# A convolution block on one core: all held tiles as native fp32 products, a grouped first norm, twelve convolution tiles on TensorE and the output gate's modulation on VectorE

## The chip, the cores and the metric

The kernel runs on one core of a Trainium2 chip. The metric is the device time of one execution in microseconds. TensorE (PE) multiplies, VectorE (DVE), ScalarE (ACT) and GpSimd (POOL) do elementwise work, SyncE (SP) issues nearly all DMA transfers. Each engine works through its own instructions in order.

## The reference

One decoder layer in fp32 for 256 positions of width 2048 (batch 1); the layer's mixer is the convolution, so the attention mixers of the reference do not run. Cut to what is computed:

```python
cond = silu(c)
mod = cond @ mod_w + mod_b                       # 6 x 2048 numbers
sh1, sc1, g1, sh2, sc2, g2 = split(mod, 6)
h = rms_norm(x, norm1_g) * (1 + sc1) + sh1
a, gt = split(h @ w_in + b_in, 2)                # 2048 -> 2 x 2048
u = a * sigmoid(gt)
u = depthwise_causal_conv(u, dw_w) + dw_b        # 31 taps along the sequence, each channel for itself
u = silu(layer_norm(u, ln_g, ln_b))
x = x + (1 + g1) * (u @ w_out + b_out)
h = rms_norm(x, norm2_g) * (1 + sc2) + sh2
x = x + (1 + g2) * (square(relu(h @ w1)) @ w2)   # 2048 -> 8192 -> 2048
```

## The kernel before

Channels lie on the 128 partitions (`P`), positions (`T` = 256) along the free axis; a vector of 2048 channels is 16 tiles of 128 (`KT`). Weights arrive in pieces of 1 MiB (128 x 2048 fp32), each loaded once, in the order of the list `order`, through a ring of five buffers named `raw` (`RAW`). `take(key)` (L182) hands out the next piece and issues the load that has room now; all loads stand in one queue on SP, so a load whose buffer is not free holds up those behind it. An order within an engine is set by a scheduler that works with a modelled time line; `urgent()` raises an instruction's priority and `issue_after` puts one behind another.

**Products.** Most of the matmul work is done as three products in the reduced type fp32r. `split_w` (L191) copies a weight half to `hi` on ACT (L200) and makes `lo = w - hi` on DVE or POOL (L201); the ring of `hi` and `lo` holds six halves, a job uses four. `mm` (L211) then multiplies `hi` with the activations' high and low part side by side (512 columns, L223) and `lo` with the high part (256 columns, L224). A *native* product instead multiplies fp32 by fp32 in one call (two records of the trace each).

**Stages.** `jobs` lists 16 in-projection jobs (`in`, a pair of a and gate tiles each), 8 out-projection jobs (`out`) and 4 x (8 `up` + 8 `down`) for the MLP.

1. *The first norm and the held tiles.* Squares of x on ACT (L433), 16 sums over channels by products with a matrix of ones (`column_sum`, L319), then an inverse root (`rms_factor`, L335). The first eight in-jobs are not done job by job: their 16 output tiles are *held* in all of PSUM, and the loop over the input tile k (L506) adds one input tile to all 16. Step k needs the modulation's scale and shift columns for k (`mod_col`, L294: one DVE instruction over 128 x 2048 that multiplies a piece of `mod_w` by `cond` and sums, L299) and one piece `first`. Steps in `NATIVE` (ten of 16) use native products (L486); in the six others `first_hi` and `first_lo` (L452, L466) split the piece on ACT and DVE, and three products follow (L490 to L492). `act_low` (L501) makes the low part of the activations for the later jobs.
2. *In-jobs 8 to 15.* Each is 32 pairs of `mm` calls. Beside them the depthwise convolution runs. A tile on DVE takes 31 multiply-adds (`tap`, L552), drawn from a stream by `advance(n)` with the counts of `ADVANCE`. A tile in `PE_TILES` goes to TensorE: `copy_wide` (L637) makes 16 shifted copies of 32 partitions each, on ACT or shared with DVE, `make_diag` (L650) builds small diagonal matrices on POOL, and `pe_conv` (L661) runs 32 products in 32-column groups, four side by side (L669). `CONV_AT` names the job behind which a tile is convolved, `COPY_AT` the job in which it is copied; the rings of copies and diagonals hold two tiles. Here also the modulation's `G1` and `SC2` parts are computed on TensorE as *row chunks* (`mod_chunk`, L232; 16 for each part, four for each of the first jobs by `LATE_IN`), and `mod_finish` (L281) turns the rows into columns by small products (L288).
3. *The tail of the convolution and the layer norm.* `stats` sums the convolved tiles and their squares on TensorE (L614); `find_shift` (L598) takes out a common mean estimated from two tiles; tile 15 is convolved last (L771), and mean and factor follow (L800 to L807).
4. *Out-jobs and the MLP*, ending with the store.

POOL makes the `lo` halves of the in-jobs (and of two out-jobs), DVE those of the rest.

```python
37  NATIVE = (1, 3, 5, 6, 8, 9, 11, 12, 14, 15)
44  PE_TILES = (0, 1, 2, 9, 10, 12, 14, 15)
45  CONV_AT = {9: (0,), 10: (1,), 11: (2,), 12: (9,), 13: (10,), 14: (12,), 15: (14,)}
46  ADVANCE = {7: 24, 8: 34, 9: 34, 10: 34, 11: 34, 12: 32, 13: 37, 14: 99}
51  LATE_IN = [0] * 8 + [4, 4, 4, 4, 4, 3, 3, 6]
299 nc.vector.scalar_tensor_tensor(w, w, 1.0, cb, op0=ALU.mult, op1=ALU.mult, accum_out=acc)
486 step = nc.tensor.matmul(p, parts_of[:, j, :], h, start=begin, stop=end, skip_group_check=True)
```

## Time and profile before

| what | value |
|---|---|
| median of 3 runs | 1124.56 us (1124.52 to 1125.03) |
| the profiled execution, its own time | 1122.33 us |
| its span | 1120.5 us, 17425 instructions |
| PE busy | 1098.4 us (98%) |
| DVE busy | 768.0 us (69%) |
| ACT busy | 582.0 us (52%) |
| POOL busy | 166.6 us (15%) |
| read from HBM | 290.14 MB |

The span is the stretch between the first and the last recorded event; the execution's own time holds 1.8 us more. A row of a time line or of a group gives start, duration, engine, source line, operation, the tile written and the tiles read with partitions x elements, and in brackets how long the engine had stood idle and what released it. Matmuls are pipelined: a record's duration holds its way through the array, so costs are taken from start to start.

### The profile page before, as it was taken

The page shows a single profiled execution, that of the slowest core. Times are in us where ns is not written, and L with a number is a line of the kernel's source. Part 1 is how long each engine was busy: PE and PEld are TensorE (multiplying, and loading weights), DVE is VectorE, ACT ScalarE, POOL GpSimd, SP SyncE. Part 2 cuts the span into 40 slices and gives each one's busy share as a digit, 9 for nine tenths or more (in the row PEclk, how much of TensorE's full clock was granted, in tenths as well). Part 3 has the DMA queues.
Part 4 walks back from the last instruction along what each step waited for, and adds up shares of the span by engine and source line. Part 5 has one row for each costly group of instructions (what it writes and reads, how often), then busy time and mean ns, then how long its engine had stood idle before and what let it go on. Part 6 is the DMA issues. An engine that isn't in the chain of part 4 may idle for free.

```text
span 1120.5 us, 17425 instructions
## 1 busy us (share of the span) xinstructions
PE 1098.4 (98%) x7088; PEld 946.6 (84%) x7088; DVE 768.0 (69%) x1025; ACT 582.0 (52%) x806; POOL 166.6 (15%) x103
## 2 busy tenths in 40 slices
PE   6999999999999999999999999999999999999998
PEld 4888776766699998888888888888888888888888
DVE  3988689987489989887765555555555665555653
ACT  5222395664675587554445554444655444555441
POOL 0000086467533262000000000000000000000000
PEclk8999999999999999999999999999999999999999
DMA  9999979888599977888775555555554655555640
GB/s 384 420 421 420 418 307 346 349 322 318 207 390 350 371 283 276 290 350 299 273 259 192 190 193 194 193 191 193 189 190 165 211 188 188 188 188 188 209 139 29
DMA packets 41553, 293.35 MB, mean 262 GB/s; under 512 B 4609, under 2 KB 5121, under 8 KB 6401
## 3 DMA queue, kind: packets, MB, share of 16 engines
q1 hardware_dynamic: 41328, 292.17, 70.4%
q8 instruction: 55, 0.90, 0.3%
q14 instruction: 24, 0.20, 0.0%
q10 hardware_dynamic: 146, 0.08, 0.0%
HBM read 290.14 MB, written 2.10 MB: 261 GB/s over the span
## 4 chain that ended last, share of the span: by engine, by line
PE 86%; DMA 6%; DVE 6%; ACT 1%; issue 0%; POOL 0%; DVEq 0%; ACTq 0%; POOLq 0%
PE mm L223 45%; PE mm L224 24%; DMA raw<-mod_c 4%; PE mm L220 3%; DVE raw L299 3%; PE mm L219 3%; PE mm L221 3%; PE row L241 2%; PE mm L669 2%; DMA raw<-w_in 1%; PE small L319 1%; DVE lo L470 1%; PE mm L111 1%; PE mm L486 1%; PE acc L669 0%
## 5 line engine op out<-in xcount | busy, mean ns | idle before, releaser
L200 ACT ACTIVATE hi<-raw 128x1024 fp32r<-128x1024 f32 x320 | 335.3, 1057 | 355.9 <-PE mm L223 327.1
L201 DVE TENSOR_TENSOR lo<-raw,hi 128x1024 fp32r<-128x1024 f32 x272 | 333.6, 1232 | 234.4 <-ACT hi L200 233.4
L223 PE MATMUL mm<-hl,hi 128*128 128x512 f32 x1184 | 414.3, 393 | 0.4 <-DVE u L686 0.4
L223 PE MATMUL mm<-u,hi 128*128 128x512 f32 x1056 | 366.8, 390 | 0.0
L224 PE MATMUL mm<-hl,lo 128*128 128x256 f32 x1184 | 332.2, 281 | 0.0
L224 PE MATMUL mm<-u,lo 128*128 128x256 f32 x1056 | 297.7, 282 | 0.0
L223 PEld LDWEIGHTS mm<-hl,hi 128*128 128x128 f32 x1184 | 221.6, 187 | 58.2 <-issue 8.4
L223 PEld LDWEIGHTS mm<-u,hi 128*128 128x128 f32 x1056 | 198.2, 188 | 41.7 <-DVE small L332 0.2
L224 PEld LDWEIGHTS mm<-hl,lo 128*128 128x128 f32 x1184 | 223.7, 189 | 5.1 <-issue 4.2
L224 PEld LDWEIGHTS mm<-u,lo 128*128 128x128 f32 x1056 | 199.6, 189 | 0.1
L299 DVE SCALAR_TENSOR_TENSOR raw<-raw,cond 128x2048 f32<-128x2048 f32 x64 | 148.3, 2320 | 20.3 <-DMA raw<-mod_c 14.7
L201 POOL TENSOR_TENSOR lo<-raw,hi 128x1024 fp32r<-128x1024 f32 x48 | 118.1, 2482 | 198.0 <-ACT hi L200 198.0
L561 DVE SCALAR_TENSOR_TENSOR acc<-u,v,acc 128x256 f32<-128x256 f32 x224 | 94.7, 490 | 1.9
L220 PE MATMUL mm<-hl,hi 128*128 128x256 f32 x288 | 81.5, 284 | 0.8 <-DVE hl L209 0.8
L219 PE MATMUL mm<-hl,hi 128*128 128x256 f32 x288 | 80.5, 284 | 1.2 <-ACT hl L208 0.8
L221 PE MATMUL mm<-hl,lo 128*128 128x256 f32 x288 | 81.1, 283 | 0.0
L219 PEld LDWEIGHTS mm<-hl,hi 128*128 128x128 f32 x288 | 54.6, 192 | 2.8 <-ACT hl L208 1.7
L220 PEld LDWEIGHTS mm<-hl,hi 128*128 128x128 f32 x288 | 55.2, 192 | 1.6 <-DVE hl L209 1.2
L221 PEld LDWEIGHTS mm<-hl,lo 128*128 128x128 f32 x288 | 55.2, 192 | 0.0
L646 ACT ACTIVATE wide<-u 32x284 f32<-32x284 f32 x110 | 48.2, 438 | 2.7 <-DVE u L686 1.4
L423 ACT ACTIVATE two<-mm 128x512 f32<-128x512 f32 x70 | 40.9, 584 | 13.5 <-PE mm L224 13.5
L523 ACT ACTIVATE two<-two,modc,amp 128x256 f32<-128x256 f32 x16 | 9.6, 599 | 71.2 <-DVE modc L279 71.2
(166 smaller groups left out, 916.7 us busy)
## 6 DMA issues: line engine op xcount, KB each, us to landing
raw<-w SPq DMA_DIRECT2D x128, 1024.0 KB, 4.9
raw<-mod_c SPq DMA_DIRECT2D x64, 1024.0 KB, 10.8
raw<-mod_r SPq DMA_DIRECT2D x32, 1024.0 KB, 7.9
raw<-w_in SPq DMA_DIRECT2D x16, 1024.0 KB, 7.2
raw<-w_out SPq DMA_DIRECT2D x16, 1024.0 KB, 7.4
first<-w_first SPq DMA_DIRECT2D x15, 1024.0 KB, 16.1
x<-x SPq DMA_DIRECT2D x2, 1024.0 KB, 6.9
x<-x SPq DMA_DIRECT2D x1, 2048.0 KB, 9.8
```

The source lines that it names most:

```text
L200: nc.scalar.activation(hi, w[:, ks, :], AF.Copy)
L201: end = engine.tensor_tensor(lo, w[:, ks, :], hi.bitcast(F32), op=ALU.subtract)
L219: nc.tensor.matmul(out_p, w, m[:, 0:T], start=begin, stop=False)
L220: nc.tensor.matmul(out_p, w, m[:, T : 2 * T], start=False, stop=False)
L221: state["mm_end"] = nc.tensor.matmul(out_p, lo[:, k % HALF, :], m[:, 0:T], start=False, stop=end)
L223: nc.tensor.matmul(p[:, c, :], hi[:, k % HALF, :], m, start=(k == 0), stop=(k == KT - 1))
L224: state["mm_end"] = nc.tensor.matmul(p[:, c, T : 2 * T], lo[:, k % HALF, :], m[:, 0:T], start=False, stop=(k == KT - 1), skip_group_check= ...
L241: state["row_end"] = nc.tensor.matmul(row_ps[0][32 * k : 32 * k + 32, :], cz[:, 4 * kg + k, 3 - b : 35 - b], w[:, 4 * k : 4 * k + 4, :], s ...
L299: nc.vector.scalar_tensor_tensor(w, w, 1.0, cb, op0=ALU.mult, op1=ALU.mult, accum_out=acc)
L423: nc.scalar.activation(t1, p[:, cs, T : 2 * T], AF.Copy)
L561: nc.vector.scalar_tensor_tensor(out, s, w, acc, op0=ALU.mult, op1=ALU.add)
L646: nc.scalar.activation(dst, src, AF.Copy)
```

## The change

- Every held tile uses native products; `first_hi`, `first_lo`, `NATIVE` and the split products go.
- The first norm's sum: half of the squares are made on DVE; the 16 sums go into four groups of 32 PSUM partitions, and one copy and one more product fold them. The first two columns are computed after the squares, and the inverse root's table is loaded earlier.
- `PE_TILES` grows from eight tiles to twelve: 0 to 2 and 7 to 15. DVE convolves tiles 3 to 6 only. `CONV_MID` sets three convolutions (1, 7, 13) into the middle of jobs 9, 10 and 15. The convolution's product is written into a free half of the PSUM tile `small` instead of an `mm` tile; the sums of `stats` move to an `acc` tile.
- `G1` is computed by 16 columns on DVE (`COLS_IN`, spread over jobs 8 to 14 between the taps); only `SC2` stays with row chunks (`ROWS_IN`: 1, 1, 1, 2, 2, 2, 1 and 6).
- `stats` for the first two groups of tiles come one job apart. The table of tap weights moves to a pool that is freed, and the pad grows by as much.

```diff
-NATIVE = (1, 3, 5, 6, 8, 9, 11, 12, 14, 15)
-GROUPS = [[4 * w + b for b in range(4)] for w in (G1, SC2)]
+GROUPS = [[4 * SC2 + b for b in range(4)]]
...
+COLS += [w * KT + k for w in (G1, SH2, G2) for k in range(KT)]
...
-PE_TILES = (0, 1, 2, 9, 10, 12, 14, 15)
-CONV_AT = {9: (0,), 10: (1,), 11: (2,), 12: (9,), 13: (10,), 14: (12,), 15: (14,)}
-ADVANCE = {7: 24, 8: 34, 9: 34, 10: 34, 11: 34, 12: 32, 13: 37, 14: 99}
+PE_TILES = (0, 1, 2, 7, 8, 9, 10, 11, 12, 13, 14, 15)
+CONV_AT = {8: (0,), 9: (2,), 10: (8,), 11: (9,), 12: (10,), 13: (11,), 14: (12,), 15: (14,)}
+CONV_MID = {9: 1, 10: 7, 15: 13}
+COPY_AT = {8: (0, 1), 9: (2, 7), 10: (8,), 11: (9,), 12: (10,), 13: (11,), 14: (12,)}
+ADVANCE = {7: 26, 8: 26, 9: 24, 10: 24, 11: 99}
 SHIFT = 2
-COPY_AT = {8: 0, 9: 1, 10: 2, 11: 9, 12: 10, 13: 12}
-PADDING = 8
-UNSHIFTED = 7
-LATE_IN = [0] * 8 + [4, 4, 4, 4, 4, 3, 3, 6]
+PADDING = 264
+ROWS_IN = {8: 1, 9: 1, 10: 1, 11: 2, 12: 2, 13: 2, 14: 1, 15: 6}
+COLS_IN = {8: 1, 9: 2, 10: 2, 11: 2, 12: 3, 13: 3, 14: 3}
...
-    dwq_sb = const.tile([P, 32 * len(PE_TILES)], F32, name="dwq_sb")
...
+    dwq_sb = early.tile([P, 32 * len(PE_TILES)], F32, name="dwq_sb")
...
+    table(AF.Abs_reciprocal_sqrt, cond[:, KT - 1, 0:1])
...
+    def rms_factor(total, ms, r, times=1):
+        by = 1.0 / (times * D)
+        nc.vector.tensor_scalar(ms, total, by, None, op0=ALU.mult)
+        return inverse_root(ms, total, by, r)
...
-    late = [("mod", nb, kg) for nb in ROWS for kg in range(4)] + [("col", SH2 * KT + k) for k in range(KT)]
+    rows_late = [("mod", nb, kg) for nb in ROWS for kg in range(4)]
+    late = [("col", w * KT + k) for w in (G1, SH2) for k in range(KT)]
...
-    quota = {("in", i): n for i, n in enumerate(LATE_IN)}
+    quota = {("in", i): n for i, n in COLS_IN.items()}
...
+    rows_of = {}
+    for n, job in enumerate(jobs):
+        n = ROWS_IN.get(n, 0)
+        rows_of[job], rows_late = rows_late[:n], rows_late[n:]
...
-        order += after[job]
+        order += rows_of[job] + after[job]
...
-    mods(by_col(0))
     p = ps.tile([P, 512], F32, name="small", bufs=1)
     for k2 in range(HALF):
         s = two()
-        nc.scalar.activation(s, pair_of(xs, k2), AF.Square)
-        column_sum(p[:, 0:T], [s[:, j, :] for j in range(2)], k2 == 0, k2 == HALF - 1)
-    r1 = tmp.tile([P, T], F32, name="r", bufs=1)
-    rms_factor(p[:, 0:T], p[:, T : 2 * T], r1)
-
-    root_end = state["root_end"]
+        if k2 < HALF // 2:
+            nc.scalar.activation(s, pair_of(xs, k2), AF.Square)
+        else:
+            nc.vector.tensor_tensor(s, pair_of(xs, k2), pair_of(xs, k2), op=ALU.mult)
+        for j in range(2):
+            g = (2 * k2 + j) % 4
+            nc.tensor.matmul(p[32 * g : 32 * g + 32, 0:T], ones[:, 0:32], s[:, j, :], start=k2 < 2, stop=k2 >= HALF - 2)
+    mods(by_col(0))
+    with urgent():
+        part = two()[:, 0, :]
+        nc.scalar.activation(part, p[:, 0:T], AF.Copy)
+        p = ps.tile([P, 512], F32, name="row", bufs=1)
+        nc.tensor.matmul(p[:, 0:T], ones, part, start=True, stop=True)
+        r1 = tmp.tile([P, T], F32, name="r", bufs=1)
+        rms_factor(p[:, 0:T], p[:, T : 2 * T], r1, 32)
...
-    first_parts = {}
-
-    def first_hi(k):
-        w = take(("first", k))
-        if k in NATIVE:
-            first_parts[k] = w
-            return
-        first_parts[k] = []
-        for h in range(2):
-            js = slice(h * HELD, (h + 1) * HELD)
-            hi = wts.tile([P, HALF, P], F32R, name="hi", bufs=6)
-            lo = wts.tile([P, HALF, P], F32R, name="lo", bufs=6)
-            with tc.issue_after(root_end):
-                nc.scalar.activation(hi, w[:, js, :], AF.Copy)
-            first_parts[k].append((hi, lo, w[:, js, :]))
-
-    def first_lo(k, h):
-        if k in NATIVE:
-            return
-        hi, lo, w = first_parts[k][h]
-        in_order(lambda: nc.vector.tensor_tensor(lo, w, hi.bitcast(F32), op=ALU.subtract))
...
     def first_mm(k, h):
+        w = take(("first", k))
         with tc.issue_after(state["step_end"].ins) if k else ExitStack():
-            parts_of = first_parts.pop(k)
-            m = hl[k // 2][:, k % 2, :]
             for n in range(HELD):
                 for c in range(2):
-                    p = held[n][:, c, :]
-                    j = 2 * n + c
-                    begin, end = k == 0 and c == 0, k == KT - 1
-                    if k in NATIVE:
-                        step = nc.tensor.matmul(p, parts_of[:, j, :], h, start=begin, stop=end, skip_group_check=True)
-                        continue
-                    hi, lo = parts_of[j // HELD][0:2]
-                    j %= HELD
-                    nc.tensor.matmul(p, hi[:, j, :], m[:, 0:T], start=begin, stop=False, skip_group_check=True)
-                    nc.tensor.matmul(p, hi[:, j, :], m[:, T : 2 * T], start=False, stop=False, skip_group_check=True)
-                    step = nc.tensor.matmul(p, lo[:, j, :], m[:, 0:T], start=False, stop=end, skip_group_check=True)
+                    step = nc.tensor.matmul(
+                        held[n][:, c, :], w[:, 2 * n + c, :], h, start=k == 0 and c == 0, stop=k == KT - 1, skip_group_check=True
+                    )
         state["step_end"] = step
...
-            first_lo(k - 1, 1)
-            if k - 1 not in NATIVE:
-                first_mm(k - 1, None)
...
-        first_hi(k)
-        if k in NATIVE:
-            first_mm(k, h)
+        first_mm(k, h)
...
-        for dst in (state["small"][:, T : 2 * T], state["shift"]):
-            nc.scalar.activation(dst, p, AF.Copy, scale=-1.0 / (SHIFT * P))
+        nc.scalar.activation(state["shift"], p, AF.Copy, scale=-1.0 / (SHIFT * P))
...
                 state["stats_end"] = nc.tensor.matmul(
-                    state["small"][32 * g : 32 * g + 32, 0:T], ones[:, 0:32], t, start=first, stop=m in last,
+                    state["sums"][32 * g : 32 * g + 32, :], ones[:, 0:32], t, start=first, stop=m in last,
...
     def stats(b):
+        if b == 0:
+            state["sums"] = ps_two()[:, 0, :]
...
-        p = ps.tile([P, 2, 2 * T], F32, name="mm", bufs=2)[:, 0, 0:T] if sq is None else ps_two()[:, 0, :]
+        p = state["small"][:, T : 2 * T] if sq is None else ps_two()[:, 0, :]
...
-            if ct == 14:
+            if HELD <= ct < KT - 1:
                 nc.vector.scalar_tensor_tensor(cv(ct), p, col("dwb", ct), state["shift"], op0=ALU.add, op1=ALU.add)
...
+    state["small"] = ps.tile([P, 512], F32, name="small", bufs=1)
     advance(ADVANCE[HELD - 1])
...
-        for ct in CONV_AT.get(n, ()) + ((15,) if n == KT - 1 else ()):
+        for ct in ((CONV_MID[n],) if n in CONV_MID else ()) + CONV_AT.get(n, ()) + ((15,) if n == KT - 1 else ()):
             make_diag(ct)
...
-        if n in COPY_AT:
-            copy_wide(COPY_AT[n], False)
+        for ct in COPY_AT.get(n, ()):
+            copy_wide(ct, False)
...
-            rows = list(after[job]) if i < KT - 1 else []
+            rows = list(rows_of[job]) if i < KT - 1 else []
             for c in range(2) if i < KT - 1 else (1, 0):
                 for ks in (range(HALF), range(HALF, KT)):
                     mm(p, c, job + (c,), hl, ks, i == KT - 1)
                     with tc.issue_after(state["mm_end"].ins):
                         mods(rows[:1])
                     del rows[:1]
+                    if n in CONV_MID and ks == range(HALF, KT) and c == (1 if i == KT - 1 else 0):
+                        with tc.issue_after(state["mm_end"].ins):
+                            pe_conv(CONV_MID[n])
...
-                if i >= KT - 2:
+                if i >= KT - 3:
                     copy_wide(i)
             if n == KT - 4:
                 add_shift(cvs[0], 4)
-                add_shift(cvs[1][:, 0:3, :], 3)
-            if n == KT - 2:
-                add_shift(cvs[2][:, 1:3, :], 2)
-            if n == KT - 1:
-                add_shift(cvs[3][:, 0:1, :], 1)
...
-                    mix(ct)
-            advance(ADVANCE.get(n, 0))
-            if n == KT - 2:
+                    pe_conv(ct)
+            if n == HELD + 1:
+                with tc.issue_after(state["conv_end"].ins):
+                    find_shift()
+            cols = list(after[job])
+            taps = ADVANCE.get(n, 0)
+            for left in range(len(cols), -1, -1):
+                m = taps // (left + 1)
+                advance(m)
+                taps -= m
+                mods(cols[:1])
+                del cols[:1]
+            if n == KT - 4:
+                add_shift(cvs[1], 4)
+            if n in (KT - 3, KT - 2):
                 with tc.issue_after(state["mm_end"].ins):
-                    for b in range(2):
-                        stats(b)
+                    stats(n - KT + 3)
...
-                nc.scalar.activation(sums, state["small"][:, 0:T], AF.Copy)
+                nc.scalar.activation(sums, state["sums"], AF.Copy)
```

25 lines of the change are left out of this document (5 added, 20 removed).

## The prediction

> **What bounds the kernel now.** I read the slices and queues of the page first, then busy time by stage, then the chain that ended last, and last the time lines of each engine around two borders: where the eight held tiles end (141 us) and where the convolution's tail begins (286 us). Columns of the first table: stretch, its length, busy time of PE, PEld, DVE, ACT and POOL with instruction counts, granted clock, DMA share, GB/s.
>
> ```profile
> span 1120.5 us, 17425 instructions
> core 0: us, PE busy (x) PEld busy (x) DVE busy (x) ACT busy (x) POOL busy (x), PEclk, DMA share, GB/s
> 4.00:128.00 124.00, 111.08 (x588) 95.66 (x587) 100.42 (x136) 38.18 (x60) 0.00 (x0) 0.97 1.01 420
> 128.00:141.00 13.00, 13.00 (x62) 11.44 (x61) 3.88 (x7) 6.19 (x10) 3.68 (x2) 1.00 1.02 417
> 141.00:286.00 145.00, 144.62 (x1179) 101.17 (x1178) 123.05 (x292) 93.30 (x167) 98.46 (x52) 1.00 0.82 316
> 286.00:308.00 22.00, 20.50 (x235) 12.02 (x234) 11.63 (x24) 15.58 (x31) 11.78 (x10) 1.00 0.67 254
> 420.00:1116.00 696.00, 696.00 (x4047) 616.58 (x4046) 427.79 (x458) 350.57 (x419) 7.40 (x3) 1.00 0.60 208
> ```
>
> There are three regimes. To 128 us the DMA engines are full (share 1.01, 420 GB/s) while PE has holes: this stage is paid in bytes. From 141 to 286 us PE is busy 144.62 of 145 us and DMA at 0.82: paid in TensorE work. The MLP from 420 us is PE alone, 696 of 696 us. The diff touches the first two; of the MLP it only moves addresses (the pad grows by the 256 elements that `dwq_sb` gave up), and I cost that at zero. The stretch 308 to 420 runs the same program from the same five `raw` buffers and I let it move as a block.
>
> **Front: all held tiles native.** Removed: six steps' ACT copies and DVE `lo` subtractions, and the waits for them. Bytes stay, so the question is how far PE ends behind the last byte.
>
> ```profile
> 124.97 0.38 PE acc L492
> 127.15 3.45 PE mm L486 x16
> 134.06 3.45 PE mm L486 x16
> 140.10 0.86 PE row L486 x4
> 286.29 3.59 PE mm L669 x64
> 109.18 2.29 DVE L299 SCALAR_TENSOR_TENSOR raw<-raw,cond 128x2048 f32<-128x2048 f32 x1 [1.57 <-DMA raw<-mod_c]
> 116.75 2.29 DVE L299 SCALAR_TENSOR_TENSOR raw<-raw,cond 128x2048 f32<-128x2048 f32 x1 [2.27 <-DMA raw<-mod_c]
> 123.70 1.22 DVE L470 TENSOR_TENSOR lo<-first,hi 128x1024 fp32r<-128x1024 f32 x1
> 127.64 2.29 DVE L299 SCALAR_TENSOR_TENSOR raw<-raw,cond 128x2048 f32<-128x2048 f32 x1
> 130.16 0.60 ACT L523 ACTIVATE two<-two,modc,amp 128x256 f32<-128x256 f32 x1 [5.23 <-DVE modc L279]
> ```
>
> The first five rows are the chain; the fifth, a whole convolution tile on PE (32 grouped products, two records each), is used further down. Step 13 is split and held by `lo` (123.70 on DVE), so its second half starts at 124.97; native step 14 starts at 127.15, step 15 at 134.06, and that ends at 140.10 + 0.86 = 141.0. A native step thus takes 134.06 - 127.15 = 6.9 us. The DVE rows that waited for DMA are the scale columns of steps 13 and 14: 7.57 us apart. That is the pace of delivery of 3 MiB, about 2.5 us each. 6.9 is below 7.5, so PE in native steps keeps pace, with 0.6 us a step to spare.
>
> Now the new end. Step 15's scale column lands at 116.75 + 7.5 = 124.3, its shift column 2.5 later, 126.8. Before, DVE began that column at 127.64, late, and `h` was ready at 130.16 + 0.60 = 130.8; the 0.8 us off makes it 129.9. Step 14's `h` comes 7.5 earlier, 122.4, its step runs to 129.3, so step 15 starts when `h` does: 129.9 + 6.9 = 136.8. **Gain 4.1 us.** What is late next are job 8's weights: behind the shift column stand 1 MiB of first weights, 0.7 of vectors and 1 MiB of w_in, 2.7 x 2.5 = 6.7 us, so 133.5. An estimate from the pace above; a copy and a subtraction must follow:
>
> ```profile
> 136.19 1.99 ACT L200 ACTIVATE hi<-raw 128x1024 fp32r<-128x1024 f32 x2
> 163.43 9.45 POOL L201 TENSOR_TENSOR lo<-raw,hi 128x1024 fp32r<-128x1024 f32 x4 [3.60 <-ACT hi L200]
> ```
>
> 1.0 for one `hi`, 9.45/4 = 2.4 for one `lo`: 136.9. I take **-4.0 us**. Bounds: zero if PE cannot hold 6.9 a step, -5 if step 15's bytes come 1 us early (the wait at 109.18 was 1.57).
>
> **Head: the first norm's sum.** Sixteen full sums become four groups side by side, half the squares go to DVE, a copy and one matmul fold them, and the table load moves ahead; DVE's first two columns stand behind its four squares, and SP's next loads behind those columns' buffers.
>
> ```profile
> 13.74 2.29 DVE L299 SCALAR_TENSOR_TENSOR raw<-raw,cond 128x2048 f32<-128x2048 f32 x1 [3.94 <-ACT cond L112]
> 9.63 9.88 PE L319 MATMUL small<-two,ones 128*128 128x256 f32 x32
> 20.06 1.28 ACT L326 ACT_TABLE_LOAD   x1 [5.31 <-DVE small L336]
> 25.61 0.80 PE L490 MATMUL mm<-hl,hi 128*128 128x256 f32 x2 [6.10 <-ACT hl L526]
> ```
>
> By the convolution tile, 32 grouped products of this width take 3.59 us, so sixteen take 1.8 of the 9.88, and the 1.28 goes; step 0 starts, as an estimate, 3 to 6 us before 25.61. The squares put ahead of DVE's columns cost nothing: the first column waited for `cond` until 13.74 anyway. The saving is **zero at the end**: it lies under the full DMA queue. It is cover, though: from 25.61, sixteen native steps end at 25.61 + 110.4 = 136.0, only 0.8 us before the bytes allow.
>
> **In stage: PE.** Sixteen row chunks (the G1 group) leave TensorE with their fold, four convolution tiles come. `mm` stays.
>
> ```profile
> 242.59 0.39 PE L223 MATMUL mm<-hl,hi 128*128 128x512 f32 x1
> 242.91 1.07 PE L241 MATMUL row<-raw,cz 128*32 128x512 f32 x8
> 243.91 0.39 PE L224 MATMUL mm<-hl,lo 128*128 128x256 f32 x1
> 234.85 0.50 PE L223 MATMUL mm<-hl,hi 128*128 128x512 f32 x1
> 242.24 0.40 PE L223 MATMUL mm<-hl,hi 128*128 128x512 f32 x1
> 242.47 0.28 PE L224 MATMUL mm<-hl,lo 128*128 128x256 f32 x1
> 224.02 0.79 PE row L288 x8
> ```
>
> A pair of `mm` matmuls takes (242.59 - 234.85)/22 = 0.352 us, a job of 32 pairs 11.3. From a 512-wide `mm` to its follower are 242.47 - 242.24 = 0.23 us in a plain run, so the chunk costs 243.91 - 242.59 - 0.23 = 1.09 us, not the 0.99 that a chain piece shows. Ahead of 286 us: 26 - 10 = 16 chunks x 1.09 = -17.4, the fold -0.8, and from six to ten convolution tiles, 4 x 3.6 = +14.4. **-3.8 us; I take -3.4**, since convolutions set into the middle of a job pay borders. The Trainium skill, "TensorEngine Tiling (Array Packing)", Key Properties, says that a change of tiling mode, not only of tile, drains TensorE. The trace agrees: 0.1 us a chunk above its bare time. By bare times the term would be 16 x 0.99 = 15.8, and the sum -2.2.
>
> **In stage: ACT, DVE, POOL.**
>
> ```profile
> 168.32 0.60 ACT L423 ACTIVATE two<-mm 128x512 f32<-128x512 f32 x1 [2.12 <-PE mm L224]
> 170.75 0.47 ACT L684 ACTIVATE two<-mm,v 128x256 f32<-128x256 f32 x1 [1.84 <-DVE mm L424]
> 173.66 0.47 ACT L677 ACTIVATE cv<-mm,v 128x256 f32<-128x256 f32 x1 [2.43 <-PE mm L669]
> 174.03 7.18 ACT L646 ACTIVATE wide<-u 32x284 f32<-32x284 f32 x16
> 144.84 5.58 DVE L561 SCALAR_TENSOR_TENSOR acc<-u,v,acc 128x256 f32<-128x256 f32 x14
> 24.00 2.22 DVE raw L299 x2
> 172.85 1.90 POOL L654 TENSOR_TENSOR diag<-v,dwq_sb 128x1024 f32<-128x1024 f32 x1
> ```
>
> DVE: four tiles less, 4 x 31 x 0.40 = -50; sixteen G1 columns, 16 x (2.22 + 0.2) = +39; tile 13's share of copies and the evacuations +7. Even. Its lateness holds `raw` buffers, hence SP's queue and the next weights, but five buffers reach a job ahead. ACT takes the load: 7.18 us for each copied tile, and five tiles (0, 1, 2, 7, 8) are due within jobs 8 to 10. PE needs there 3 x 11.3 + 3 x 1.09 + 5 x 3.6 = 55.2 us. ACT needs 5 x 7.18 = 35.9, three jobs' `hi` 12 x 1.0 = 12, the second pair of job 8 at 2.0, evacuations and gates 3 x 1.07 = 3.2, four convolution evacuations 1.9 and some held gates 2.5: 57.5 us. **+2 us**, bounds 0 and +19 (see the rivals). From job 11 one tile a job remains, and ACT has room. In the tail conv 14 and the sums still cover the copy of tile 15: zero.
>
> **Sum.** On the profiled execution, 1122.33 us with a span of 1120.5: -4.0 - 3.4 + 2.0 = -5.4, to 1116.9. The median of the runs, 1124.56, lies 2.2 above that execution, so 1119.2.
>
> **Rivals.**
> ACT hides its 2 us, because a late convolution is placed behind the next job's matmuls: for it speaks that `mm`'s two buffers are no longer shared with convolutions. 1124.56 - 7.4 = 1117.2.
>
> The front does not shorten: native steps lose 0.3 us each to jitter and PE ends at 141 as now. For it: only 0.8 us of cover without the head's gain. Against: the 6.9 is itself measured. 1123.2.
>
> The two-input lock. Here the trace shows:
>
> ```profile
> 313.50 2.29 DVE L299 SCALAR_TENSOR_TENSOR raw<-raw,cond 128x2048 f32<-128x2048 f32 x1 [0.74 <-PE mm L221]
> 314.49 6.91 POOL L201 TENSOR_TENSOR lo<-raw,hi 128x1024 fp32r<-128x1024 f32 x2 [4.33 <-ACT hi L200]
> ```
>
> Two `lo` in 6.91 us instead of 4.8, beginning while DVE ran a column: POOL stood until the column ended. If each G1 column holds POOL for 2.22 us, jobs 12 and 13 need 9.45 + 1.9 + 3 x 2.22 = 18.0 us of POOL against 11.3 + 2 x 1.09 + 3.6 = 17.1 of PE, job 14 18.0 against 16.0: +3.8 if no lead is left, 1123.0. The Trainium skill, "SBUF — State Buffer", section "SBUF: two separate sides", gives this as a rule: a DVE instruction with two SBUF inputs and a reading GpSimd one exclude each other for their whole length; the pair of rows above agrees. Against the price: POOL starts most jobs with `lo` already ahead.
>
> The slower side: ACT stays in order through its waits. In job 9 it stood 2.12 + 1.84 + 2.43 = 6.4 us for PE, for DVE's addition and for the convolution, when it had nothing else to do. Where all of it is demanded, the same stops in three jobs are 19.2 us. The point that decides: above 5.4 us of them (under a third) nothing is gained. At three fifths, +11.5: 1130.7.
>
> **How the numbers follow.** Forecast 0.45, ACT hidden 0.20, lock 0.10, front as before 0.08, ACT's stops 0.17. A difference under 0.2% (2.2 us) is about what runs of this kernel cannot tell from none. Forecast and hidden ACT are faster by more, 0.65; the lock and the unshortened front lie within it, 0.18; the stops are slower, 0.17. The range runs from 1115.0 (both bounds of the front and of ACT, with a little of the tail) to 1126.5, into the nearer part of the stops.
>
> **What would show it.** The step-15 group of native matmuls ends near 137 and the first `mm` of job 8 follows at once; DVE waits for `mod_c` in nearly every step from about 9 on; job 15's last `mm` lies near 281; the MLP keeps its length. Wrong: ACT's stops in jobs 8 to 10 with PE idle before L669; POOL `lo` means above 2.6; holes of PE ahead of L486 at the end of the front; an MLP longer by over 1 us, which I gave no cause for.

## The result, and the profile after

The kernel became slower: 1139.29 us (1135.98 to 1140.48) against 1124.80 us for the kernel before on the same chip, a ratio of 1.0109 with a 95% interval of [1.0064, 1.0154]. The forecast was 1119.2. The profiled execution of the changed kernel took 1140.48 us, its span is 1137.3 us.

The same table by stage, for the changed kernel. The stages end at other times now: the held tiles at 137.5, the in-stage at 298.

```profile
span 1137.3 us, 17448 instructions
core 0: us, PE busy (x) PEld busy (x) DVE busy (x) ACT busy (x) POOL busy (x), PEclk, DMA share, GB/s
4.00:128.00 124.00, 114.18 (x511) 93.49 (x510) 90.54 (x128) 25.19 (x46) 0.00 (x0) 0.97 1.01 420
128.00:137.50 9.50, 9.50 (x46) 8.28 (x44) 3.88 (x9) 5.30 (x11) 1.84 (x1) 1.00 1.03 421
137.50:298.00 160.50, 148.02 (x1305) 104.85 (x1307) 140.02 (x220) 116.24 (x219) 128.40 (x56) 0.98 0.77 294
298.00:320.00 22.00, 18.25 (x216) 9.99 (x216) 11.94 (x20) 13.38 (x28) 12.58 (x9) 1.00 0.61 215
434.00:1130.00 696.00, 694.68 (x4028) 614.57 (x4028) 427.92 (x459) 351.05 (x419) 7.85 (x4) 1.00 0.59 208
```

The front is shorter by 3.5 us (141.0 to 137.4). The in-stage, which was 145 us with PE idle for 0.4, is 160.5 us with PE idle for 12.5; POOL's busy time went from 98 to 128 us with 56 instructions against 52. From here on I measure to one mark, the first row product of the MLP's first job (L256 before, L258 after, 128 products in one row of the chain), and to the end. For the kernel before, the chain's row and the stretch from the held tiles to it:

```profile
406.97 3.63 PE row L256 x128
...
141.00:406.97 265.97, 263.10 (x2209) 209.73 (x2211) 225.91 (x408) 174.32 (x298) 144.67 (x79) 1.00 0.85 324
```

The same two for the changed kernel:

```profile
421.83 3.63 PE row L258 x128
...
137.50:421.83 284.33, 267.45 (x2330) 214.79 (x2332) 246.47 (x336) 197.15 (x349) 175.46 (x84) 0.98 0.82 308
```

The mark is 14.9 us later, the stretch behind it 2.0 us longer (715.5 against 713.5). Between the front and the mark PE is idle for 284.33 - 267.45 = 16.9 us, before for 2.9. Nearly all of the 14.9 us are lost ahead of the out-jobs: the first product of out-job 0 starts at 305.31 us before and at 319.49 us now, 14.2 us later, and from there to the mark it takes 101.7 and 102.3 us.

What grew is seen in the groups of the in-stage (137.5 to 300 us; mean ns behind the busy time), first of the kernel before:

```profile
L201 POOL TENSOR_TENSOR lo<-raw,hi 128x1024 fp32r<-128x1024 f32 x38 | 90.1, 2394 | 182.1 <-ACT hi L200 182.1
L644 DVE COPY wide<-u 32x284 f32<-32x284 f32 x18 | 8.4, 466 | 0.4
L561 DVE SCALAR_TENSOR_TENSOR acc<-u,v,acc 128x256 f32<-128x256 f32 x224 | 94.7, 490 | 1.9
```

Of the changed kernel, and as last row its one-element addition in the front (4 to 137 us), where POOL does nothing:

```profile
L203 POOL TENSOR_TENSOR lo<-raw,hi 128x1024 fp32r<-128x1024 f32 x37 | 107.2, 2923 | 165.8 <-ACT hi L202 165.7
L301 DVE SCALAR_TENSOR_TENSOR raw<-raw,cond 128x2048 f32<-128x2048 f32 x16 | 44.5, 2783 | 8.4 <-DMA raw<-mod_c 8.4
L281 DVE TENSOR_TENSOR modc<-modc,v 128x1 f32<-128x1 f32 x16 | 23.0, 1438 | 0.2
L618 DVE COPY wide<-u 32x284 f32<-32x284 f32 x19 | 11.5, 604 | 0.3
L536 DVE SCALAR_TENSOR_TENSOR acc<-u,v,acc 128x256 f32<-128x256 f32 x112 | 45.4, 479 | 0.0
...
L281 DVE TENSOR_TENSOR modc<-modc,v 128x1 f32<-128x1 f32 x16 | 2.5, 158 | 0.5
```

Adding one number to each partition takes 158 ns in the front and 1438 ns here. Columns take 2783 instead of 2290 ns, `lo` 2923 instead of 2394. The convolution's taps, whose accumulator lies in PSUM, are as before (479 and 490 ns). DVE's time line, and POOL's below it, show the pattern:

```profile
233.11 2.29 DVE L301 SCALAR_TENSOR_TENSOR raw<-raw,cond 128x2048 f32<-128x2048 f32 x1
235.44 2.22 DVE L281 TENSOR_TENSOR modc<-modc,v 128x1 f32<-128x1 f32 x1
237.59 2.28 DVE L301 SCALAR_TENSOR_TENSOR raw<-raw,cond 128x2048 f32<-128x2048 f32 x1
239.91 2.24 DVE L281 TENSOR_TENSOR modc<-modc,v 128x1 f32<-128x1 f32 x1
```

```profile
233.86 8.28 POOL L203 TENSOR_TENSOR lo<-raw,hi 128x1024 fp32r<-128x1024 f32 x2 [3.06 <-ACT hi L202]
```

POOL's first `lo` stands until the column ends at 235.4, and runs to 237.6; the addition, issued at 235.44, ends with it; then the next column runs, POOL's second `lo` stands, and the next addition ends with that. In this stretch the two engines take strict turns, and the turn is paid by an instruction that would last 0.16 us. The Trainium skill, "SBUF — State Buffer", section "SBUF: two separate sides", says that a DVE instruction with two SBUF inputs, or in a fast copying mode, and a GpSimd instruction that reads SBUF exclude each other for their whole length; the trace agrees for the columns and the additions, and for the copies (below) as far as their length shows it, and the taps with an input in PSUM (0.48 us) stay out of it.

DVE's lateness then holds the `raw` buffers, and SP's queue with them. From the waits of SP's queue between 180 and 215 us (us in total, times, longest):

```profile
SPq L182 <- DVE raw L301: 13.7, 3, 7.9
```

How much this path costs is not shown. Over the whole in-stage the columns hold the queue for 31.6 us and POOL's `lo` for 99.1; before, `lo` held it for 92.2 and PE's row chunks for 38.2, with no hole of PE over 0.4 us.

PE pays in holes, that is stretches without a matmul. Five of its nine over 0.7 us, on its time line (two more, of 1.65 and 1.88 us at 182 and 191 us, wait for ACT):

```profile
221.82 1.06 PE L243 MATMUL row<-raw,cz 128*32 128x512 f32 x8 [1.70 <-DMA raw<-mod_r]
244.40 1.06 PE L243 MATMUL row<-raw,cz 128*32 128x512 f32 x8 [1.82 <-DMA raw<-mod_r]
273.21 0.39 PE L221 MATMUL mm<-hl,hi 128*128 128x256 f32 x1 [3.46 <-ACT hi L202]
306.00 4.09 PE L643 MATMUL acc<-wide,diag 128*32 128x256 f32 x61 [2.25 <-DVE wide L618]
516.38 0.50 PE L225 MATMUL mm<-u,hi 128*128 128x512 f32 x1 [1.27 <-DVE two L431]
```

After the longest its clock is granted at half for 6.8 us, from 273.7 on (column PEclk, third from the right):

```profile
276.00:278.00 2.00, 2.00 (x21) 1.00 (x24) 0.01 (x1) 1.96 (x3) 2.00 (x2) 0.50 1.00 422
```

### The profile page after: what moved, and what is told of

The parts are those of the page before. It is cut to its first block, busy times and chain, and to the rows that moved or that the text cites. A ratio compares the mean times of both kernels' runs of the same rounds, so it can differ in the third digit from the quotient of the medians.

```text
span 1137.3 us, 17448 instructions
## 1 busy us (share of the span) xinstructions
PE 1102.6 (97%) x7114; PEld 946.2 (83%) x7114; DVE 778.2 (68%) x946; ACT 590.5 (52%) x843; POOL 195.7 (17%) x107
## 4 chain that ended last, share of the span: by engine, by line
PE 66%; DMA 14%; DVE 12%; ACT 4%; issue 3%; DVEq 0%; ACTq 0%; SPq 0%
PE mm L225 35%; PE mm L226 19%; DMA raw<-mod_c 12%; DVE raw L301 5%; PE mm L222 3%; PE mm L221 3%; PE mm L223 3%; ACT wide L620 2%; DVE acc L536 2%; DMA raw<-w_in 1%; DVE modc L281 1%; DVE lo L203 1%; ACT hi L202 1%; PE small L643 1%; DMA v<-vec 1%
## 5 line engine op out<-in xcount | busy, mean ns | idle before, releaser
L301 DVE SCALAR_TENSOR_TENSOR raw<-raw,cond 128x2048 f32<-128x2048 f32 x80 | 192.8, 2413 | 52.6 <-DMA raw<-mod_c 51.4
L203 POOL TENSOR_TENSOR lo<-raw,hi 128x1024 fp32r<-128x1024 f32 x48 | 135.5, 2849 | 183.1 <-ACT hi L202 183.0
L620 ACT ACTIVATE wide<-u 32x284 f32<-32x284 f32 x165 | 72.2, 438 | 9.3 <-DVE u L660 7.3
L474 PE MATMUL mm<-two,first 128*128 128x256 f32 x256 | 60.0, 389 | 8.8 <-ACT two L502 8.8
L474 PEld LDWEIGHTS mm<-two,first 128*128 128x128 f32 x256 | 49.4, 195 | 17.6 <-ACT two L502 10.8
```

The lines of the kernel that those rows point to most:

```text
L203: end = engine.tensor_tensor(lo, w[:, ks, :], hi.bitcast(F32), op=ALU.subtract)
L474: step = nc.tensor.matmul(held[n][:, c, :], w[:, 2 * n + c, :], h, start=k == 0 and c == 0, stop=k == KT - 1, skip_group_check=True)
L620: nc.scalar.activation(dst, src, AF.Copy)
```

## The experiments

One table first, for orientation. First out is the start of the first product of out-job 0. Idle is PE's idle time from the end of the held tiles to the mark, busy its busy time there, MLP the stretch from the mark to the end of the span, all from the profiled execution; time is the median of the runs and the ratio is to the kernel before, run beside it on the same chip.

| kernel | first out | mark | idle | busy | MLP | time | ratio [95%] |
|---|---|---|---|---|---|---|---|
| before | 305.3 | 406.97 | 2.9 | 263.1 | 713.5 | 1124.8 | |
| changed | 319.5 | 421.83 | 16.9 | 267.4 | 715.5 | 1139.3 | 1.0109 [1.0064, 1.0154] |
| e1_front | 301.8 | 406.88 | 5.1 | 264.3 | 717.7 | 1125.3 | 1.0002 [0.9983, 1.0022] |
| e8_native | 301.6 | 407.55 | 4.7 | 265.4 | 714.4 | 1124.0 | 0.9994 [0.9979, 1.0009] |
| e2_nolock | 308.9 | 411.01 | 12.3 | 261.2 | 713.6 | 1129.5 | 1.0034 [1.0014, 1.0055] |
| e3_batch | 317.2 | 419.53 | 14.2 | 267.9 | 715.5 | 1138.4 | 1.0106 [1.0073, 1.0139] |
| e4_copies | 317.9 | 422.20 | 19.2 | 265.5 | 714.9 | 1139.3 | 1.0124 [1.0084, 1.0163] |
| e5_rows | 326.6 | 432.45 | 10.4 | 284.5 | 714.1 | 1149.0 | 1.0227 [1.0213, 1.0241] |
| e6_short | 314.2 | 419.06 | 15.0 | 266.5 | 717.8 | 1136.7 | 1.0125 [1.0100, 1.0150] |
| e7_early | 319.1 | 421.48 | 15.0 | 269.0 | 714.9 | 1138.6 | 1.0142 [1.0124, 1.0161] |
| e12_nog1 | 316.0 | 422.66 | 16.6 | 268.6 | 717.3 | 1138.0 | 1.0121 [1.0099, 1.0142] |
| e16_halflo | 314.9 | 420.83 | 15.8 | 267.6 | 715.1 | 1139.2 | 1.0131 [1.0109, 1.0153] |
| e11_shortlo | 305.0 | 410.94 | 10.8 | 262.6 | 718.1 | 1129.1 | 1.0033 [1.0017, 1.0050] |
| e15_shortcop | 300.2 | 404.92 | 5.8 | 261.6 | 713.6 | 1122.8 | 0.9981 [0.9966, 0.9996] |
| e14_all | 299.4 | 401.19 | 2.9 | 260.8 | 714.6 | 1119.3 | 0.9945 [0.9923, 0.9966] |
| e9_poollo | 301.7 | 404.97 | 3.3 | 264.1 | 717.2 | 1121.5 | 0.9961 [0.9940, 0.9983] |
| e10_seven | 300.2 | 403.44 | 3.6 | 262.4 | 720.1 | 1125.6 | 1.0007 [0.9995, 1.0019] |
| e13_pad | 300.6 | 403.92 | 3.4 | 263.0 | 715.4 | 1120.8 | 0.9942 [0.9923, 0.9961] |

My theory (A) was the exclusion of DVE and POOL; the rivals were ACT's copies (B) and the columns' place behind the taps, which holds `raw` buffers and SP's queue (C).

### The lock

**e2_nolock**: the G1 columns read their second input from PSUM, and one addition replaces sixteen (G1's values are not the reference's).

```diff
+    other = state["small"][:, None, 0:P].to_broadcast([P, KT, P])
-    nc.vector.scalar_tensor_tensor(w, w, 1.0, cb, op0=ALU.mult, op1=ALU.mult, accum_out=acc)
+    nc.vector.scalar_tensor_tensor(w3, w3, 1.0, other, op0=ALU.mult, op1=ALU.mult, accum_out=acc)
...
```

> The changed kernel with the second operand of the sixteen G1 columns read from PSUM instead of SBUF (so G1 is another number), and their sixteen additions of the bias replaced by one at the end. DVE's work, the order, the loads and the ring stay. Theory A, the lock of DVE's two-input instructions against GpSimd: columns fall from 2.78 us to about 2.3, POOL's lo from 2.9 to 2.4, the in-stage from 160.5 us to 144 to 148, total 1121 to 1125. Theory B, ACT is the bound with its nine copied tiles: nothing changes, 1136 to 1140. Theory C, columns stand behind the taps and hold raw buffers, SP's queue and the next weights: within 4 us of the changed kernel, since DVE's work and order stay.

Columns took 2280 ns, `lo` 2397, and the mark came 10.8 us earlier, the first out-product 10.6. The time, 1129.5 us, lies between what A (1121 to 1125) and what B and C had said. Part of what stays is the experiment's own: the columns now read the PSUM bank into which the convolution writes, and PE waited 3.56 us there. The copies still met POOL's `lo` (nine took 7.9 and 9.2 us).

**e3_batch**: only the sixteen one-element additions become one.

```diff
-        elif which != SH2:
+        elif which not in (SH2, G1):
             return mod_bias(at, 1, acc)
```

> The changed kernel with only the sixteen one-element additions of the bias taken out of the stage and done by one instruction ahead of the layer norm; the result is the same. Theory A: the additions (1.44 us each instead of 0.16) gave DVE 20 of its 28 us of waiting, so 4 to 10 us come back, 1129 to 1135. Theory B: nothing, 1136 to 1140. Theory C: at most 3 us, since the additions hold no raw buffer themselves.

The orders of PE and POOL are unchanged, the 23 us of additions are gone, and the mark moves by 2.3 us only; the time, 1138.4 us, is what B and C had said, not A (1129 to 1135). Columns now take 3480 ns on average. The waiting moved to the next DVE instructions that read SBUF beside POOL; nine copies, too, took 14.66 us there instead of 6.76.

**e11_shortlo**: the other side of the lock. POOL's `lo` halves of the in-jobs are made an eighth as long, and the products read that one block for all; POOL's order stays.

```diff
+            n = 1 if key[0] == "in" else HALF
-            end = engine.tensor_tensor(lo, w[:, ks, :], hi.bitcast(F32), op=ALU.subtract)
+            end = engine.tensor_tensor(lo[:, 0:n, :], w[:, h * HALF : h * HALF + n, :], hi[:, 0:n, :].bitcast(F32), op=ALU.subtract)
...
```

> The changed kernel with POOL's lo halves of the in-jobs cut to an eighth (128 of 1024 columns; the lo products then use one block of weights for all, so a and gate are off in their low part); columns and their loads stay. Lock theory: columns fall to 2.28 to 2.35 us and one-element adds to 0.16, DVE is 28 us shorter, PE's idle from front to MLP marker falls from 16.9 to under 6 us and its busy time from 267.5 to 262, marker 403 to 408. If the columns' place in the loads (SP's queue behind DVE) costs by itself: idle stays over 10 and the marker at 412 to 417.

Columns took 2307 ns and additions 517, not 158: the lock is short here and not gone, since the diagonals and the `lo` of the two out-jobs keep their length. The mark is 10.9 us earlier than in the changed kernel, between the two forecasts (403 to 408 and 412 to 417). Idle stayed at 10.8, not under 6, which had been named as the sign for C.

That the mark moves as far as from DVE's side does not mean that both took away the same. The first out-product, in the kernel before, the changed one and e11_shortlo:

```profile
305.31 0.50 PE L219 MATMUL mm<-hl,hi 128*128 128x256 f32 x2 [0.80 <-ACT hl L208]
...
319.49 0.50 PE L221 MATMUL mm<-hl,hi 128*128 128x256 f32 x2 [1.40 <-ACT hl L210]
...
305.00 0.50 PE L222 MATMUL mm<-hl,hi 128*128 128x256 f32 x2 [1.39 <-ACT hl L211]
```

Here the gain is 14.5 us. From there to the mark e11_shortlo takes 105.9 us instead of 102.3: reached earlier, the out stage gets a hole of 2.47 us and 6.8 us at half clock behind it, which the changed kernel doesn't have (see the front by itself). So the lock is the largest part of the loss, 14.5 of the 20.1 us that lie here between the changed kernel and e14_all (below), not all.

**e12_nog1** leaves out G1's columns and their loads; **e16_halflo** makes `lo` of every second in-job piece on DVE. Both keep the rest.

```diff
-COLS_IN = {8: 1, 9: 2, 10: 2, 11: 2, 12: 3, 13: 3, 14: 3}
+COLS_IN = {}
```

```diff
-                split_w(job + (c,), nc.gpsimd if on_pool else nc.vector)
+                split_w(job + (c,), nc.gpsimd if on_pool and (c == 0 or job[0] == "out") else nc.vector)
```

> The changed kernel without G1's columns and their 16 MiB of loads (G1 is then its bias alone); twelve convolution tiles stay. If the twelve tiles by themselves are harmless, as the prediction had it, PE is held by its own work: marker 399 to 403 and time 1115 to 1119. If the conv tiles' waits (one PSUM half for all, late copies) cost: idle of PE over 6 us and marker 406 to 410.

> The changed kernel, complete, with lo of every second weight piece of the in-jobs made on DVE (1.2 us each) instead of POOL (2.4): half as many POOL instructions for columns, additions and copies to meet, 18 more DVE instructions of 1.2 us. Lock theory: DVE's waiting halves (28 to about 14 us) and pays for the 22 us of new work in part; POOL is free half the time; columns 2.4 to 2.6, additions under 0.8, marker 414 to 418, time 1130 to 1134. If DVE's length is the bound and not the waiting: marker 424 or later.

e12_nog1 missed both of its values by over 12 us, and e16_halflo, with 420.8, came 2.8 above that of the lock theory. Up to the first out-product they gain 3.5 and 4.5 us, and the out stage (106.7 and 105.9 us) takes all or most of it back. The time lines show what else held them. DVE and PE of e12_nog1:

```profile
269.86 14.14 DVE L618 COPY wide<-u 32x284 f32<-32x284 f32 x9
284.02 0.48 DVE L649 SCALAR_TENSOR_TENSOR cv<-small,v,shift 128x256 f32<-128x256 f32 x1
...
284.65 6.32 PE L643 MATMUL small<-wide,diag 128*32 128x256 f32 x64 [8.31 <-DVE cv L649]
```

POOL beside them:

```profile
269.45 1.93 POOL L628 TENSOR_TENSOR diag<-v,dwq_sb 128x1024 f32<-128x1024 f32 x1
271.32 4.91 POOL L203 TENSOR_TENSOR lo<-raw,hi 128x1024 fp32r<-128x1024 f32 x2
276.19 1.97 POOL L628 TENSOR_TENSOR diag<-v,dwq_sb 128x1024 f32<-128x1024 f32 x1
278.13 4.76 POOL L203 TENSOR_TENSOR lo<-raw,hi 128x1024 fp32r<-128x1024 f32 x2
```

The same copies, and what PE waits for behind them, in e16_halflo:

```profile
279.37 15.05 DVE L618 COPY wide<-u 32x284 f32<-32x284 f32 x9
...
295.09 5.10 PE L643 MATMUL small<-wide,diag 128*32 128x256 f32 x60 [6.24 <-DVE cv L649]
```

Nine copies take 2.82 us where POOL does nothing (at 262.5 us in the changed kernel), 4.26 to 4.42 us in the kernel before and 14.1 to 15.1 us beside such a run of POOL. Behind them in DVE's order stands the evacuation of a convolution tile, and the next tile's products wait for that, because all evacuated tiles share one half of `small`. So PE stood 8.3 us, and then ran the tile in 6.3 instead of 3.7 us at half clock. In the changed kernel the columns and additions carry most of the waiting, and the copies of that tile take 6.76 us; without columns, or with fewer `lo` on POOL, the copies carry it. Removing one victim hands the lock to the next.

**e6_short** cuts each G1 column to 128 elements and makes one addition of sixteen; **e5_rows** takes G1 back to TensorE and keeps twelve convolution tiles.

```diff
+            n = P if which == G1 else D
-            nc.vector.scalar_tensor_tensor(w, w, 1.0, cb, op0=ALU.mult, op1=ALU.mult, accum_out=acc)
+            nc.vector.scalar_tensor_tensor(w[:, 0:n], w[:, 0:n], 1.0, cb[:, 0:n], op0=ALU.mult, op1=ALU.mult, accum_out=acc)
...
```

```diff
-GROUPS = [[4 * SC2 + b for b in range(4)]]
+GROUPS = [[4 * w + b for b in range(4)] for w in (G1, SC2)]
-ROWS_IN = {8: 1, 9: 1, 10: 1, 11: 2, 12: 2, 13: 2, 14: 1, 15: 6}
+ROWS_IN = {8: 4, 9: 4, 10: 4, 11: 4, 12: 4, 13: 3, 14: 3, 15: 6}
-COLS_IN = {8: 1, 9: 2, 10: 2, 11: 2, 12: 3, 13: 3, 14: 3}
+COLS_IN = {}
...
```

> The changed kernel with each G1 column cut from 2048 to 128 elements (G1 is then wrong) and one addition for all; the loads and their order stay. Lock theory: as the kernel without the lock, marker near 411, if the 4 us left there are ring, ACT or job order. If they are DVE's own time (16 columns of 2.28 us, 36 us of DVE), the marker falls to 406.97 - 3.5 - 3.4 = 400 to 403 and the time to 1118 to 1121, which is what the prediction forecast.

> The changed kernel with G1 back on TensorE's row chunks (16 chunks and their fold return, about 18 us of PE), all twelve convolution tiles kept; no column runs on DVE beside POOL's lo. If columns against lo is the whole of the loss: PE has no holes over 1 us in the stage, lo mean 2.4, one-element adds gone, and the MLP's first marker lies at before's 406.97 - 3.5 (front) + 14.4 (four tiles) = 418, against 421.8 of the changed kernel, in spite of 18 us more PE work; time about 1135. If four more tiles on ACT and in job order cost waits of their own, the 4 us that were left without the lock come on top: 422 and about 1139.

Neither is clean, since the scheduler, which works with modelled times, set other orders. In e6_short PE waited 3.98 us for a row weight behind SP's queue; in e5_rows it ran without a hole to 289 us, then stood 6.11 us for the same evacuation, behind copies that took 12.2 us. Both marks were 8 us and more above what either theory had said; they count for the copies' share, and against the lock of columns as the only cause.

### The rivals: ACT's copies and the columns' place

**e4_copies**: ACT makes 4 wide copies instead of 16 narrow ones of a tile (the convolution of those tiles is not the reference's). **e7_early** gives the G1 columns a raised priority ahead of the taps.

```diff
+        if not both:
+            for g in range(4):
+                nc.scalar.activation(wides[ct][:, g, :], u[ct][:, g : g + T + 28], AF.Copy)
+            return
```

```diff
+            with urgent():
+                mods(cols)
+            cols = []
```

> The changed kernel with ACT's sixteen shifted copies of each convolution tile replaced by four over all partitions (so those tiles are convolved wrongly): ACT's copying falls from 7.2 to about 1.9 us a tile, some 48 us less in the stage. Theory A: within 4 us of the changed kernel, 1134 to 1140, POOL's lo still near 2.9. Theory B: the stalls go, 1121 to 1126. Theory C: as A.

> The changed kernel with a job's G1 columns urgent ahead of the taps instead of spread between them: raw buffers come free sooner, the lock stays. If the loss is that columns behind taps hold the ring and SP's queue: chain without raw<-mod_c, marker 412 to 416. Lock theory: columns still meet lo, means stay at 2.7 to 3.5, marker 419 to 424.

With the lock at full length fewer copies on ACT change nothing (422.2): between 170 and 200 us PE is busy for 26.8 us instead of 25.6, but holes of 5.42 us (for a row weight) and 6.46 us (for an evacuation on DVE) follow. e7_early set no instruction of any engine elsewhere, so it says nothing about C; it is a second measurement of the changed kernel (1138.6). C, by itself, stayed untried.

**e15_shortcop** joins the short `lo` and the fewer copies; **e14_all** adds one more edit, the first `lo` half of out 2 on POOL (from e9_poollo, below).

> The changed kernel with POOL's lo halves of the in-jobs an eighth as long and ACT's copies 4 instead of 16 (convolution wrong), the out stage as it was. Against the kernel with short lo alone (marker 410.9) this takes away ACT's queue, against the kernel with all three taken away (401.2) it leaves the hole in the out stage. If ACT's queue carries its share by itself: PE without holes over 1 us at 170 to 200 us, marker 404 to 406.5. If the out stage's hole is nearly all of it: marker 408 to 411.

> The changed kernel with three suspected costs taken away together: POOL's lo halves of the in-jobs an eighth as long (the lock), ACT's copies of a convolution tile 4 instead of 16 (the convolution of those tiles is then wrong), and the first lo half of out 2 on POOL (the hole in the out stage). The lock alone gave 10.9 of 14.9 us at the MLP's marker. If the rest is ACT's queue between 170 and 200 us and that hole: no PE hole over 1 us there, marker 400 to 404, MLP 713.5 to 716, time 1115 to 1120. If ACT's queue is hidden: marker 406 to 408.

Once POOL's `lo` is short, ACT is the next bound: the mark goes from 410.9 to 404.9, the first out-product from 305.0 to 300.2. From 170 to 200 us PE had waited for ACT's evacuations behind copies; first the stretch in e11_shortlo, then in e15_shortcop:

```profile
170.00:200.00 30.00, 25.00 (x238) 17.54 (x240) 28.61 (x58) 28.42 (x59) 10.28 (x9) 1.00 0.75 281
```

```profile
170.00:200.00 30.00, 30.00 (x289) 19.76 (x282) 30.00 (x67) 13.71 (x26) 8.22 (x8) 1.00 0.71 256
```

The hole in the out stage then carries another 3.7, and with all three edits the mark is 401.19 and the time 1119.34. From the held tiles to the mark:

```profile
137.50:401.19 263.69, 260.76 (x2330) 212.17 (x2332) 224.25 (x335) 147.70 (x241) 107.10 (x83) 1.00 0.87 332
```

e14_all has the same 2330 matmul records as the changed kernel, but 260.8 us of PE instead of 267.4. The changed kernel runs at a granted clock of 0.50 for 6.8 us from 273.7 and for 3.4 us from 321.5, e14_all never, so 5.1 of these 6.7 us are the lower clock behind holes; the other 1.6 were not traced. The 20.6 us between the two marks are 14.0 of holes and 6.7 of longer work. Nine copies beside full `lo` of an out-job still take 12.9 us in e14_all; PE has no wait behind them there.

### The front by itself

**e8_native** is the kernel before with all held tiles native; **e1_front** adds the grouped norm.

```diff
-NATIVE = (1, 3, 5, 6, 8, 9, 11, 12, 14, 15)
+NATIVE = tuple(range(16))
```

> The kernel before with native held tiles alone, the first norm's sum as before. The prediction says that the head is only cover: front ends at 136.8 to 137.7 as with the grouped sum, 3.5 us before 141, time as with both (1125.3, 1.000). If sixteen native steps from 25.6 need the earlier start, PE ends near 139 to 141 and conv 14 near 285.

> The kernel before with the front of the change alone: native held tiles and the grouped first norm; in-stage, convolution and G1 as before. If the front earned what the trace of the changed kernel shows (it ended at 137.4 us instead of 141.0), the time falls by 3 to 4 us, to about 1121, and the in-stage keeps its 145 us. If that saving is given back later (the layer norm's start or the MLP), it stays at 1124.5.

In both the front ends 3.2 to 3.3 us earlier and the in-stage keeps its length: the first out-product comes 3.5 and 3.7 us earlier. In both nothing of it reaches the mark. The grouped norm adds nothing that the times show. The gain is lost in the out stage (105.1 and 105.9 us instead of 101.7), here on the time lines of DVE, POOL and PE in e8_native, and in the stretch behind:

```profile
314.09 3.27 DVE L201 TENSOR_TENSOR lo<-raw,hi 128x1024 fp32r<-128x1024 f32 x1 [1.81 <-ACT hi L200]
...
310.78 5.50 POOL L201 TENSOR_TENSOR lo<-raw,hi 128x1024 fp32r<-128x1024 f32 x2 [4.30 <-ACT hi L200]
...
318.02 0.39 PE L220 MATMUL mm<-hl,hi 128*128 128x256 f32 x1 [2.47 <-DVE hl L209]
```

```profile
320.00:325.00 5.00, 5.00 (x25) 5.00 (x25) 0.93 (x3) 1.02 (x1) 0.00 (x0) 0.50 0.71 254
```

Three us earlier, DVE's `lo` of out 2 falls beside POOL's second `lo` and takes 3.27 us instead of the 1.35 of before; the activation splits behind it are late; PE stands 2.47 us and then runs at half clock for 6.8 us. **e9_poollo** makes that one half on POOL:

```diff
+            by = nc.gpsimd if key == ("out", 2, 0) and h == 0 else engine
-            end = engine.tensor_tensor(lo, w[:, ks, :], hi.bitcast(F32), op=ALU.subtract)
+            end = by.tensor_tensor(lo, w[:, ks, :], hi.bitcast(F32), op=ALU.subtract)
```

> All held tiles native, nothing else of the change, and the first lo half of out 2, which stood on DVE ahead of two activation splits and took 3.27 us beside POOL's lo, made on POOL as the third in a row. If the front's 3.5 us were lost to the 2.47 us hole of PE at 318 and the half clock that followed it (5.8 us at 0.50, 2.9 us lost): no hole over 0.6 us there, clock 1.00, MLP marker at 402.5 to 403.5, time 1119 to 1121 (ratio 0.996). If the gain is lost to the bytes of the out stage whatever the order: marker 406 to 407.5, time unchanged.

The half clock of e8_native lasts 6.8 us, not the 5.8 read above. With the half on POOL the hole is gone (clock 1.00 from 315 to 325), the mark is 2.6 us earlier than in e8_native, and the kernel is faster than before by 0.4% [0.2, 0.6]. The mark lies between the two forecasts: of the expected 4 to 5 us, 1.3 are a hole at 329, where PE now waits for DVE, and 1.7 a stretch of 3.4 us at half clock at 303, which e8_native doesn't have.

**e10_seven** also convolves tile 2 on DVE, whose idle time was free before the change; **e13_pad** repeats it with the pad longer by the 32 elements that the table `dwq_sb` lost.

```diff
-PE_TILES = (0, 1, 2, 9, 10, 12, 14, 15)
+PE_TILES = (0, 1, 9, 10, 12, 14, 15)
-CONV_AT = {9: (0,), 10: (1,), 11: (2,), 12: (9,), 13: (10,), 14: (12,), 15: (14,)}
+CONV_AT = {9: (0,), 10: (1,), 12: (9,), 13: (10,), 14: (12,), 15: (14,)}
-ADVANCE = {7: 24, 8: 34, 9: 34, 10: 34, 11: 34, 12: 32, 13: 37, 14: 99}
+ADVANCE = {7: 28, 8: 38, 9: 38, 10: 38, 11: 38, 12: 36, 13: 41, 14: 99}
...
```

```diff
-PADDING = 8
+PADDING = 40
```

> As the kernel with that half on POOL, and tile 2 convolved on DVE instead of TensorE (seven tiles on PE; 31 taps more, spread over jobs 7 to 13). PE is the bound of the in-stage, with 22 us of DVE idle in it: PE -3.6 us, taps +12.4 us on DVE, which the idle time takes: marker 399 to 400, time about 1116. If DVE's lateness binds (a conv waits for its evacuation, weights for their buffers), the marker is 403 or later.

> As the kernel with seven tiles on TensorE, with the pad 32 elements longer, the amount by which dwq_sb had become shorter; every engine's order is the same. In the MLP of that kernel the up jobs' 512-wide matmuls take 399 ns instead of 391 (PE is never idle there) and the MLP is 720 us long instead of 713.5. If addresses behind the shorter tile are the cause: matmuls back at 391, MLP 713 to 715, marker 403.4, time 1117 to 1119 (ratio 0.993 to 0.995). If not, 1125 again.

The mark of e10_seven came at 403.44, 1.5 us ahead of e9_poollo instead of the 3.6 that I had asked of it (403 or later had been named for the case that DVE's lateness binds), and its MLP is 720.1 us long with PE never idle. A group of the MLP (600 to 1100 us) in e10_seven, then in e13_pad, whose engines run the same instructions in the same order:

```profile
L224 PE MATMUL mm<-hl,hi 128*128 128x512 f32 x717 | 253.5, 399 | 0.0
```

```profile
L224 PE MATMUL mm<-hl,hi 128*128 128x512 f32 x719 | 249.4, 391 | 0.0
```

With the pad the matmuls are back at 391 ns and the MLP at 715.4. e13_pad has the lowest time of the complete kernels here, 1120.75 us, ratio 0.9942 [0.9923, 0.9961]; the interval overlaps with that of e9_poollo.

## Why the prediction was wrong, point by point

- **Front, -4.0**: right. Step 15 was ready at 130.1 (forecast 129.9) and PE ended at 137.4 (forecast 136.9); -3.5. That the head's saving is zero at the end is right too; that it is needed as cover is not (e8_native without it ends its front as early).
- **"I let it move as a block"** (308 to 420 us): wrong in principle, and enough by itself to cancel the front. Moved 3.5 us, a DVE `lo` met POOL's; the stage gave all of it back (e1_front, e8_native), and one half moved to POOL recovered 2.6 us. In the changed kernel, which comes 14.2 us later, this hole does not appear, and the stage costs only 0.7 us more.
- **PE in the in-stage, -3.4**: mis-sized. With nothing else in the way PE's busy time to the mark fell from 263.1 to 260.8 in e14_all, -2.3; the bare times in the text gave -2.2.
- **DVE, "even"**: this is the step that failed. The columns were costed at 2.22 + 0.2 us from rows where POOL was idle. Here DVE paid (2783 - 2290) x 16 = 7.9 us in columns and (1438 - 158) x 16 = 20.5 us in additions, and POOL waited too: (2923 - 2394) x 37 = 19.6 us in `lo`. The budget of work was about right: from the held tiles to the mark DVE is busy for 225.9 us before, 246.5 in the changed kernel, and 224.3 in e14_all, where most of POOL's `lo` is short. The step left out what POOL would add to it.
- **The lock rival, 1123.0 at 0.10**: the right mechanism with the wrong price. I let columns hold POOL and gave POOL's time against PE's. I did not let POOL hold DVE, whose small instructions pay a whole `lo` each, nor follow DVE's lateness into SP's queue, nor the copies. Measured price: 10.6 us at the first out-product from DVE's side, the experiment's own hole included, and 14.5 from POOL's (10.8 and 10.9 at the mark).
- **ACT, +2, bounds 0 to +19**: 6.0 at the mark, 4.8 at the first out-product, with `lo` short (e15_shortcop against e11_shortlo), inside the bounds. The slower rival, ACT's stops, has a part of its truth, but not as the cause that decides: with `lo` at full length fewer copies gave nothing (e4_copies).
- **The tail, zero**: 2.5 us. The nine copies of tile 15 took 6.74 us instead of 4.26 beside POOL's `lo`, and PE waited 2.25 for them.
- **MLP, zero**: +2.0 us in the profiled execution (+1.4 in that of e7_early, whose order is the same); of these 1.27 are a hole at 516 that waits for DVE. What the changed addresses do there was not tried in the changed kernel; its matmuls ran at the old 391 ns.
- **Holes cost their length**: an unspoken step, wrong. 5.1 us of the loss are PE's lower clock after holes.
- The named signs did point there: the `lo` mean above 2.6 was listed as a sign of error, and it was 2.92.

That e14_all's time, 1119.3 us, equals the forecast is in part luck: of the forecast -4.0 - 3.4 + 2.0 the front gave 0.5 less and PE 1.1 less, and ACT's +2 was taken out with its copies. Its mark, 401.19, is 406.97 - 3.5 - 2.3 because PE's idle time is again that of the kernel before, 2.9 us. Open stays how much C carries alone, and how the loss divides: 10.9, 6.0 and 3.7 us by the mark, 14.5, 4.8 and 0.8 by the first out-product, and in another order of removal perhaps otherwise (ACT's share shows only when `lo` is short).

## What to carry to other kernels

Before work is moved to DVE, list every DVE instruction that would then run beside a POOL instruction reading SBUF, and cost each, the 0.16 us ones too, at up to the length of the POOL instruction; here an input in PSUM took it off the list (taps 0.48 us, columns 2.28). When a stage is to start earlier, look at which instructions of two engines will newly meet behind it, since a phase that worked by chance is lost. And repad after any change of a table's size: 128 bytes in each partition cost more here than the edit gained. When an experiment shifts a stage, measure ahead of the next stage too: the out stage took 101.7 to 106.7 us here, by when it began.
